# Weight halves of the token mixings written to memory beside an earlier stage, and a new order of the projections

## The chip, the core and the metric

The kernel runs on one core of one Trainium2 chip. The metric is the device time of one execution in microseconds (us). The engines are TensorE (PE, with its weight loads as PEld), VectorE (DVE), ScalarE (ACT), GpSimd (POOL) and SyncE (SP), which here only issues DMAs. All work is in float32; a matmul operand is held as a high part (rounded to the matmul's format) and a low part (the remainder).

## The reference

Two blocks follow one another on one sequence of 512 tokens with 1024 features. The first block is one layer (modulated norms, a gated block MLP beside an mLSTM, then a feed-forward of 4096 with a squared relu). The second is two layers, each with a feed-forward, a token mixing and another feed-forward:

```python
def second_block(x, ...):
    for l in range(DEPTH_2):
        x = x + 0.5 * swiglu(rmsnorm_2(x, ffn1_norm[l]), ...)
        x = x + token_mixing(rmsnorm_2(x, mix_norm[l]), positions, w_in[l], ...)
        x = x + 0.5 * swiglu(rmsnorm_2(x, ffn2_norm[l]), ...)
    return rmsnorm_2(x, final_norm)

def token_mixing(h, ...):
    proj = h @ w_in
    a_part, b_part, c_part = jnp.split(proj, [A_COLS, A_COLS + B_COLS], axis=-1)
    ...
```

The token mixing has three kinds of attention: four dilated heads ("a"), eight latent heads ("m", whose queries and keys come from two small normed latents `cq` and `ckv`), and four differential heads ("d", the difference of two softmaxes, then a head norm). Their outputs are concatenated and multiplied by `w_out`.

## The kernel before

Activations are feature-major: eight tiles of 128 features x 512 tokens. A product of two float32 operands is three matmuls (high x high, high x low, low x high; `mm3`, L246 to 250). A weight unit of 128 x 1024 is loaded into `wraw` (`load_weights`, a ring of 4), and `split_weights` makes the high part with a copy on ACT (L219) and the low part with a subtraction on DVE or, with `pool=True`, on POOL (L220). Both halves stand in one tile `wsp` of 2048 columns, a ring of 3. In the mixings the projections ask for POOL.

The first feed-forward of the first block (`ff`, 64 units of 24 matmuls, 515 to 881 us) loads and splits one unit ahead of each run. It runs inside a region where PE's order is the order of the code; DVE, ACT, POOL and SP are ordered by the scheduler of the tile framework.

`mix(l, ...)` is the token mixing, called once per layer, at about 1243 and 2273 us. Its projections are jobs in the order of the table `JOBS`; the jobs of `FIRST` are done before the first attention tile, and the others fill PE's time between the steps of the tiles (`pieces`, with a budget per tile from `PIECE`). `need` runs jobs at once when a tile lacks its operand. `vd` and `va` are token-major values of the d and a heads; `dq0`, `dk0`, `aq0` and so on are feature-major queries and keys; `kr` is the rotated key, `vb` the latent values, `qk0` to `qk3` the latent queries and keys. The d queries and keys are cut into quadrants on DVE and ACT (`stacked`, L1313 to 1325).

Small products of norms on PE are `toksum` (L306, sums over features), `bc_t` (L313, a transpose) and `bc_b` (L322, a broadcast). Between them lie short DVE steps and one power on POOL (`g_rsqrt`, L293). They belong to chains which emit their next step after a given amount of PE time (the tables `NORM`, `CHAIN`, `INV`), counted by `spend`. An attention tile is scores (`sc`, L1606 for the d heads), a maximum on DVE (`mn`, L1609) which frees the score bank, an exponential on ACT, for d heads the difference (`p`, L1616), a transpose (`ptr`, L1571), its split (`ptl`), and the product with the values (`pv`).

Of the kernel before, what the change touches and what calls it, by code (L numbers as in the profile page):

```python
# [11 lines left out]
F32 = mybir.dt.float32  # L12
# [3 lines left out]
ALU = mybir.AluOpType  # L16
# [56 lines left out]

HEADS = "d0 d1 a0 a1 d2 d3 a2 a3 m0 m1 m2 m3 m4 m5 m6 m7"
MIX_ORDER = [6, 7, 0, 1, 2, 3, 4, 5]
JOBS = "vd dq0 dk0 dq1 aq0 va ak0 dk1 aq1 cq0 cq1 ak1 cq2 ckv0 ckv1 kr vb qk0 qk1 qk2 qk3"
FIRST = "vd dq0 dk0 dq1 aq0"
PIECE = {"d": 2.2, "a": 2.7, "m": 0.6}
STEP = 0.4
LAG = 2  # L80
HEAD0 = 6.5
HEAD = (1.5, 1.0, 2.3, 2.0, 0.6)
ADA0 = 31.0
# [3 lines left out]
CHAIN = (4.0, 4.0, 3.3, 4.5)  # L87
END = (2.0, 1.0)
EARLY = 4
XLP = (0, 1, 2, 3, 4)  # L90
POOL1 = ("q",)
POOL2 = (True, True, False, 3)
# [51 lines left out]
            return e.value  # L144


class Net:
    def __init__(self, ctx, tc, a):
        self.tc, self.nc, self.a = tc, tc.nc, a
        nc = self.nc  # L150
        pool = lambda name, bufs, **k: ctx.enter_context(tc.tile_pool(name=name, bufs=bufs, **k))
        self.cp = pool("const", 1)
        self.wp = pool("weights", 3)
        self.big = pool("big", SLOTS)
        self.tp = pool("tmp", 7)
        self.sp = pool("small", 4)
        self.ps = pool("psum", 1, space=PSUM)
        self.extra, self.within = None, ctx.enter_context(ExitStack())
        self.psb = {"g": 3, "s": 2, "t": 2, "v": 1}
        self.small = "t"  # L160
        self.t, self.chains, self.open_block = 0.0, [], None
        self.last_load = None

        cst = self.cp.tile([P, NCST], F32, name="cst")
# [12 lines left out]
        nc.gpsimd.memset(self.mhalf, -0.5)  # L177
# [110 lines left out]
    def g_rsqrt(self, ss, scale, n, tag=None, eps=EPS):  # L288
        nc = self.nc
        ms, y, t = self.tiny("ms"), self.tiny("y", tag=tag), self.tiny("t")  # L290
        ms, y, t = ms[:, :n], y[:, :n], t[:, :n]
        nc.vector.tensor_scalar(ms, ss, scale, eps, op0=ALU.mult, op1=ALU.add)  # L292
        nc.gpsimd.tensor_tensor(y, ms, self.mhalf[:, :n], op=ALU.pow)  # L293
        yield NORM[2]
        nc.vector.tensor_tensor(t, y, y, op=ALU.mult)
        nc.vector.tensor_tensor(t, t, ms, op=ALU.mult)
        nc.vector.tensor_scalar(t, t, -0.5, 1.5, op0=ALU.mult, op1=ALU.add)
        nc.vector.tensor_tensor(y, y, t, op=ALU.mult)
        return y
# [9 lines left out]
    def g_bcast(self, f8, name, out=None, tag="small", keep=False, tiles=range(NT)):  # L309

        nc = self.nc
        pt = self.bank(tag, "bc_t")
        nc.tensor.transpose(pt[:8, :P], f8, self.c("ident"))  # L313

        self.ft = self.ft[1:] + self.ft[:1]
        ft = self.ft[0]
        nc.vector.tensor_copy(ft[:8], pt[:8, :P])
        nc.vector.tensor_tensor(ft[32:], pt[:8, :P], ft[:8].bitcast(F32), op=ALU.subtract)
        yield NORM[3]
# [12 lines left out]
    def g_bcast4(self, r, name, **k):  # L332
        f8 = self.tiny("f8")
        for h in range(2):
            self.nc.vector.tensor_copy(f8[:, 4 * h:4 * h + 4], r)
        yield NORM[4]
        return (yield from self.g_bcast(f8, name, **k))

    def sq_acc(self, acc, src, first, scale=None):
# [427 lines left out]
    def block1_rest(self, mg):  # L767
# [76 lines left out]
        def gen():  # L844
            yield 2.5
            p0, p1 = self.tok_sum(acc[0]), self.tok_sum(acc[1])
            yield 0.6
            r = yield from self.g_rsqrt(p0, 1.0 / D, NT)
            r2 = self.tiny("r2", 4)
            nc.vector.tensor_tensor(r2, p1, r, op=ALU.mult)  # L850
            nc.vector.tensor_tensor(r2, r2, r, op=ALU.mult)
            rr = yield from self.g_rsqrt(r2, 1.0 / D, NT)
            nc.vector.tensor_tensor(rr, rr, r, op=ALU.mult)
            yield 0.4
            box.rb = yield from self.g_bcast4(rr, "rb2")
# [412 lines left out]
    def mix(self, l, xs, norm, gain):  # L1268


        nc, a = self.nc, self.a
        self.small = "g"
        csc = 96.0 ** -0.5
        mixed, ready = [None] * KT, [False] * KT
        S, scored = {}, [0]

        def get(chain, name):
            while getattr(chain, name) is None:
# [4 lines left out]
        def feature(key, done):  # L1283
            def run(w):
                o = self.bank("g", key)
                yield from self.g_gemm(o, w, xs)
                yield from done(o)
            return lambda: self.weights(a["w2f"][l, FM2_AT[key]], KT, P, pool=True), run

        def scaled(key, factor=1.0):  # L1290

# [35 lines left out]
                S[key] = st  # L1327
            return feature(key, done)

        def values(name, src):  # L1330

            def run(us):
                banks = [self.bank("g", name + "a"), self.bank("g", name + "b")]
# [16 lines left out]
            return lambda: [self.weights(src[i], 4, 256, True) for i in range(2)], run  # L1350

        def latent(name, i, n, gn, last):
            def done(o):
# [41 lines left out]
        def rotated_key():  # L1395
# [9 lines left out]
            def rotation(t):  # L1405
# [5 lines left out]
                for i in range(2):  # L1411
# [5 lines left out]
            def load():  # L1417
                w = self.kilo("wpe", 2)[:, :1024].rearrange("p (k n) -> p k n", k=KT)
                raw = self.load_weights(a["w2f"][l, FM2_AT["kpe"]], KT * P)
                raw = raw.rearrange("p (k n) -> p k n", k=KT)[:, :, :64]  # L1420
                nc.scalar.activation(w[:, :, :64], raw, AF.Copy)
                nc.gpsimd.tensor_tensor(w[:, :, 64:], raw, w[:, :, :64].bitcast(F32), op=ALU.subtract)
                return w

            def run(w):

                o = self.bank("g", "kpe")
# [3 lines left out]
                    self.spend(2 * T * CYCLE)  # L1431
                    yield
                yield from done(o)
            return load, run

        def latent_values():
            def run(w):
# [11 lines left out]
            return lambda: self.weights(a["w2kv"][l], 2, T, pool=True), run  # L1449

        def latent_qk(pr):
            def run(w):
# [25 lines left out]
            return lambda: self.weights(a["w2qk"][l, pr], 1, 1024, pool=True), run  # L1478

        job = {"vd": values("vd", a["w2t"][l, 1]), "va": values("va", a["w2t"][l, 0]), "kr": rotated_key(), "vb": latent_values()}  # L1480
# [44 lines left out]
        def filler():  # L1525
            w = jobs[0][0]()
            for i, (_, run) in enumerate(jobs):
                ahead = jobs[i + 1][0]() if i + 1 < len(jobs) else None
                yield from run(w)
                w = ahead  # L1530
            yield from output()

# [124 lines left out]
        def inverse(pr):  # L1657

            yield INV[0]
            f8 = self.tiny("f8i")  # L1660
            nc.vector.reciprocal(f8, S["sum", pr])
            yield INV[1]
            S["inverse", pr] = yield from self.g_bcast(f8, "fb", tag="t")

        def add_parts(out, o, hh):
# [61 lines left out]
        n = len(tiles)  # L1727
        with self.in_order("ffn"):
            need(*FIRST.split())
        for t in range(-1, n + 3 + LAG + 1):  # L1730

            for lag in (1 + LAG, 1, 0, 1 + LAG, 3 + LAG, LAG, 2 + LAG, -1):
# [194 lines left out]
```

## Time and profile before

| What | Value |
|---|---|
| Median of 3 runs | 2974.22 us (2973.06 to 2974.68) |
| The profiled execution's own time | 2968.44 us |
| Its span, first to last instruction | 2966.7 us |
| PE busy | 2868.8 us (97%) |
| First feed-forward of the first block | 515 to 881 us |
| Head of the first mixing, to the second tile's scores | 1242.7 to 1298.3 us |
| Head of the second mixing, to the second tile's scores | 2272.6 to 2325.5 us |

The span is less than the execution's own time by what lies around the instructions, and the profiled execution is 5.8 us below the median of the runs. A busy PE is not a PE at its peak, since matmuls are pipelined and their ends are modelled; what is read here is the idle time before a matmul, what ended it, and the granted clock of a stretch.

### The profile page before, as it was taken

Reading aid. Unit: us, or ns where it says so; the run is one execution under the profiler, and the core shown is the slowest. Engines: PE = TensorE matmul, PEld = TensorE weight load, DVE = VectorE, ACT = ScalarE, POOL = GpSimd, SP = SyncE. Lnnn points to the kernel's source line nnn. Section 1 sums busy time; section 2 is a strip of 40 time slices with the busy share of each in tenths; the row PEclk is TensorE's granted clock in tenths of the full one; section 3 lists DMA queues with packets and bytes.
Section 4 is the critical chain, followed back from the end, with each engine's and each line's share of the span. In section 5 each row is a group of like instructions: output and inputs, shape, how many; then the busy total and the mean of one; then the engine's idle time right before and its main releaser. Section 6 shows DMA issues by size and latency. Waiting matters only on the chain.

```text
span 2966.7 us, 41470 instructions
## 1 busy us (share of the span) xinstructions
PE 2868.8 (97%) x16251; PEld 2459.4 (83%) x16251; DVE 2030.2 (68%) x3286; ACT 1495.7 (50%) x2527; POOL 417.6 (14%) x255
## 2 busy tenths in 40 slices
PE   6999999999999999989999999999999899999998
PEld 4888977888877999877788999889998777889997
DVE  7766565533448767678768776786775887687675
ACT  5665554422334544467664444444444777544444
POOL 4233340000000000134420000000001344100000
PEclk9999999999999999999999999999999999999999
DMA  6333432222222323211112323323323110133232
GB/s 238 113 122 125 166 111 97 84 95 97 92 93 82 117 91 107 86 65 48 39 43 88 107 95 104 106 87 103 106 90 98 59 51 29 57 96 102 95 106 65
DMA packets 88792, 278.47 MB, mean 94 GB/s; under 512 B 9835, under 2 KB 12139, under 8 KB 88596
## 3 DMA queue, kind: packets, MB, share of 16 engines
q1 hardware_dynamic: 88596, 275.83, 28.1%
q8 instruction: 127, 2.08, 0.3%
q14 instruction: 69, 0.57, 0.1%
HBM read 273.69 MB, written 2.10 MB: 93 GB/s over the span
## 4 chain that ended last, share of the span: by engine, by line
PE 68%; DVE 10%; issue 3%; ACT 3%; DMA 2%; POOL 1%; POOLq 0%; SPq 0%; DVEq 0%; ACTq 0%
PE down L248 5%; PE down L249 5%; PE down L250 5%; PE ff L248 4%; PE ff L250 4%; PE ff L249 4%; PE e L248 4%; PE e L249 4%; PE e L250 4%; PE g L250 2%; PE g L248 2%; PE g L249 2%; PE pv L1589 2%; DMA wraw<-in_w2g 2%; PE ptr L1571 1%
## 5 line engine op out<-in xcount | busy, mean ns | idle before, releaser
L219 ACT ACTIVATE wsp<-wraw 128x1024 fp32r<-128x1024 f32 (+2 forms) x400 | 358.0, 896 | 408.4 <-issue 132.7
L220 DVE TENSOR_TENSOR wsp<-wraw,wsp 128x1024 fp32r<-128x1024 f32 (+2 forms) x334 | 343.8, 1029 | 187.8 <-ACT wsp L219 187.1
L220 POOL TENSOR_TENSOR wsp<-wraw,wsp 128x1024 fp32r<-128x1024 f32 (+1 forms) x66 | 155.7, 2362 | 913.1 <-ACT wsp L219 887.6
L248 PE MATMUL down<-hid,wsp 128*128 128x512 f32 (+1 forms) x712 | 279.2, 392 | 0.0
L250 PE MATMUL down<-hid,wsp 128*128 128x512 f32 (+1 forms) x712 | 279.1, 392 | 0.0
L249 PE MATMUL down<-hid,wsp 128*128 128x512 f32 (+1 forms) x712 | 278.9, 392 | 0.0
L220 DVE TENSOR_TENSOR a<-wraw,a 128x512 fp32r<-128x512 f32 x204 | 134.2, 686 | 138.5 <-ACT a L219 138.5
L219 ACT ACTIVATE a<-wraw 128x512 fp32r<-128x512 f32 x204 | 120.5, 624 | 214.1 <-DMA wraw<-in_w2g 200.8
L293 POOL TENSOR_TENSOR y<-ms,mhalf 128x4 f32<-128x4 f32 (+2 forms) x24 | 27.4, 1140 | 1251.7 <-DVE ms L292 1251.7
L220 DVE TENSOR_TENSOR s<-s,s 128x1024 fp32r<-128x1024 f32 x136 | 163.9, 1217 | 3.9 <-ACT s L219 3.6
L250 PEld LDWEIGHTS down<-hid,wsp 128*128 128x128 f32 x712 | 133.8, 188 | 30.8
L249 PEld LDWEIGHTS down<-hid,wsp 128*128 128x128 f32 x712 | 134.0, 188 | 25.2
L248 PEld LDWEIGHTS down<-hid,wsp 128*128 128x128 f32 x712 | 133.8, 188 | 24.9
L250 PE MATMUL e<-th,s 128*128 128x256 f32 x544 | 152.6, 280 | 0.0
L249 PE MATMUL e<-tl,s 128*128 128x256 f32 x544 | 152.5, 280 | 0.0
L248 PE MATMUL e<-th,s 128*128 128x256 f32 x544 | 152.5, 280 | 0.0
L219 ACT ACTIVATE s<-s 128x1024 fp32r<-128x1024 f32 x136 | 141.1, 1051 | 18.6 <-PE gate L250 6.1
L1115 DVE SCALAR_TENSOR_TENSOR x<-down,x 128x512 f32<-128x512 f32 x158 | 108.1, 684 | 18.2 <-PE down L250 18.0
L447 POOL TENSOR_TENSOR ada<-ada,cb 128x1024 f32<-128x1024 f32 x32 | 84.4, 2651 | 169.4 <-DMA ada<-in_ada 159.0
L249 PEld LDWEIGHTS e<-tl,s 128*128 128x128 f32 x544 | 102.5, 188 | 0.0
L250 PEld LDWEIGHTS e<-th,s 128*128 128x128 f32 x544 | 102.3, 188 | 0.0
L248 PEld LDWEIGHTS e<-th,s 128*128 128x128 f32 x544 | 102.2, 188 | 0.0
(629 smaller groups left out, 8952.0 us busy)
## 6 DMA issues: line engine op xcount, KB each, us to landing
wraw<-in_w2g SPq DMA_DIRECT2D x176, 512.0 KB, 4.1
ada<-in_ada SPq DMA_DIRECT2D x48, 512.0 KB, 5.4
wraw<-in_w2d SPq DMA_DIRECT2D x96, 256.0 KB, 2.7
wraw<-in_w1f SPq DMA_DIRECT2D x44, 512.0 KB, 3.3
wraw<-in_w2d SPq DMA_DIRECT2D x64, 320.0 KB, 3.1
wraw<-in_w1a SPq DMA_DIRECT2D x32, 512.0 KB, 3.2
wraw<-in_w1b SPq DMA_DIRECT2D x32, 512.0 KB, 3.2
wraw<-in_w2f SPq DMA_DIRECT2D x28, 512.0 KB, 3.2
```

The costliest lines, as they stand in the source:

```text
L219: self.nc.scalar.activation(hi, src, AF.Copy)
L220: (self.nc.gpsimd if pool else self.nc.vector).tensor_tensor(lo, src, hi.bitcast(F32), op=ALU.subtract)
L248: mm(out, ah, bh, start=start, stop=False)
L249: mm(out, ah, bl, start=False, stop=False)
L250: mm(out, al, bh, start=False, stop=stop)
L293: nc.gpsimd.tensor_tensor(y, ms, self.mhalf[:, :n], op=ALU.pow)
L447: nc.gpsimd.tensor_tensor(s, s, self.cb, op=ALU.mult)
L1115: nc.vector.scalar_tensor_tensor(x[:, n], o, 0.5, x[:, n], op0=ALU.mult, op1=ALU.add)
L1571: nc.tensor.transpose(tr[:, b * P:(b + 1) * P], p[:, b * P:(b + 1) * P], self.c("ident"))
L1589: nc.tensor.matmul(o, values[b][:, h * P:(h + 1) * P], pt[i][:, b], start=b + i == 0, stop=b + i == NT)
```

## The change

For both layers, the weights of all jobs are loaded and split during the first feed-forward of the first block. A chain `g_parts` starts there after 30 us of PE time and, every 6 us of it, loads one unit, splits it on ACT and DVE into a tile of the `wsp` ring, and stores this tile (1 MB, for the rotated key half of it) to an array `parts` in the device's memory: 46 units. In the mixing `ready_weights` loads a pair of halves from there straight into a `wsp` tile; no split is left for the jobs (the output projection keeps its own).

The order `JOBS` is new, `FIRST` has three jobs instead of five, and `PIECE` moves filler from the a heads to the d heads. A job whose matmuls end before the norm's factor is there leaves its evacuation to a list `late`. The small products use the banks "t" up to the first tile and "g" afterwards (before, "g" all along), and inside the tile loop some of the times of their chains are 1.8 times as long (`SLACK`).

```diff
-JOBS = "vd dq0 dk0 dq1 aq0 va ak0 dk1 aq1 cq0 cq1 ak1 cq2 ckv0 ckv1 kr vb qk0 qk1 qk2 qk3"
-FIRST = "vd dq0 dk0 dq1 aq0"
-PIECE = {"d": 2.2, "a": 2.7, "m": 0.6}
+JOBS = "dq0 vd dk0 aq0 va ak0 dq1 dk1 ckv0 ckv1 aq1 cq0 cq1 cq2 ak1 kr vb qk0 qk1 qk2 qk3"
+FIRST = "dq0 vd dk0"
+PIECE = {"d": 2.4, "a": 2.5, "m": 0.6}
+PARTS = (30.0, 5.0)
...
+    def g_parts(self):
+        yield PARTS[0]
+        for l in range(2):
+            for key, src in mixing_units(self.a, l):
+                for i, s in enumerate(src):
+                    n = len(self.parts_at)
+                    raw, w = self.load_weights(s, 1024), self.kilo("wsp", 2)
...
+                        self.split(w[:, :1024], w[:, 1024:], raw)
+                    yield 1.0
+                    self.nc.sync.dma_start(out=self.parts[n][:, :w.shape[1]], in_=w.bitcast(F32))
+                    self.parts_at[l, key, i] = n
+                    yield PARTS[1]
+
+    def ready_weights(self, l, key, i, nk, n):
+        w = self.kilo("wsp", 2)
+        f = 1024 if key == "kr" else 2048
+        with self.tc.issue_after(self.last_load.ins):
+            self.last_load = self.nc.sync.dma_start(out=w[:, :f].bitcast(F32), in_=self.parts[self.parts_at[l, key, i]][:, :f])
...
     def g_rsqrt(self, ss, scale, n, tag=None, eps=EPS):
-        yield NORM[2]
+        yield NORM[2] * self.slack
...
     def mix(self, l, xs, norm, gain):
-        self.small = "g"
+        self.small = "t"
...
-                yield from done(o)
-            return lambda: self.weights(a["w2f"][l, FM2_AT[key]], KT, P, pool=True), run
+                if norm.rb is None:
+                    late.append(done(o))
+                else:
+                    yield from done(o)
+            return lambda: self.ready_weights(l, key, 0, KT, P), run
...
             need(*FIRST.split())
+        self.small, self.slack = "g", SLACK
```

The order of SyncE at the start of the first feed-forward, before (`w1a`, `w1b` are its own weights):

```order
L229 DMA wraw<-in_w1o 128x1024 x5
L229 DMA wraw<-in_w1a 128x1024 x16
L229 DMA wraw<-in_w1b 128x1024 x16
L229 DMA wraw<-in_w1a 128x1024 x16
L229 DMA wraw<-in_w1b 128x1024 x16
```

and after (`w2f`, `w2t` are weights of the mixings):

```order
L251 DMA wraw<-in_w1o 128x1024 x5
L251 DMA wraw<-in_w1a 128x1024 x6
L251 DMA wraw<-in_w2f 128x1024
L251 DMA wraw<-in_w1a 128x1024
L251 DMA wraw<-in_w2t 128x1024
L251 DMA wraw<-in_w1a 128x1024
L287 DMA parts<-wsp 128x2048
L251 DMA wraw<-in_w2t 128x1024
L251 DMA wraw<-in_w1a 128x1024
L287 DMA parts<-wsp 128x2048
```

After the sixth unit a load of the mixings' weights and a store stand beside each load of the stage's own, and this goes on to the end of the stage.

The order of POOL from the last steps of the first block into the first mixing, before:

```order
L293 TENSOR_TENSOR y<-ms,mhalf 128x4 x3
L220 TENSOR_TENSOR wsp<-wraw,wsp 128x1024 x3
L293 TENSOR_TENSOR y<-ms,mhalf 128x4
L220 TENSOR_TENSOR wsp<-wraw,wsp 128x1024 x9
L1687 TENSOR_TENSOR bias<-bias,cst 128x512 x2
L220 TENSOR_TENSOR wsp<-wraw,wsp 128x1024
```

and after:

```order
L348 TENSOR_TENSOR y<-ms,mhalf 128x4 x4
L1742 TENSOR_TENSOR bias<-bias,cst 128x512 x7
L348 TENSOR_TENSOR y<-ms,mhalf 128x8
L1742 TENSOR_TENSOR bias<-bias,cst 128x512
L348 TENSOR_TENSOR y<-ms,mhalf 128x4
```

The weight splits are gone from POOL; the powers of the norms and the sums of the a heads' biases are left.

The order of DVE ahead of the first score maximum (`ISA p,mn`) in the first mixing, before (`dq` with numbers from 10322 on is `dq1`):

```order
L1313 SCALAR_TENSOR_TENSOR qf<-dq_10322,rb 128x512
L1323 CAST dq_10349<-qf 32x512
L1323 CAST dq_10350<-qf 32x512 x2
L1319 TENSOR_TENSOR dq_10349<-qf,dq_10349 32x512 x2
L1319 TENSOR_TENSOR dq_10350<-qf,dq_10350 32x512 x2
L1325 COPY dq_10350<-dq_10350 32x512
L1294 SCALAR_TENSOR_TENSOR qf<-aq_10374,rb 128x512
L220 TENSOR_TENSOR aq_10401<-qf,aq_10401 128x512
L1609 ISA p,mn<-sc,bias 128x512
```

and after:

```order
L246 SCALAR_TENSOR_TENSOR vd_10525<-vdb,y,vd_10525 128x4x64 x2
L1373 SCALAR_TENSOR_TENSOR qf<-dk_10536,rb 128x512
L1383 CAST dk_10563<-qf 32x512
L1383 CAST dk_10564<-qf 32x512
L1379 TENSOR_TENSOR dk_10563<-qf,dk_10563 32x512 x2
L1379 TENSOR_TENSOR dk_10564<-qf,dk_10564 32x512
L1664 ISA p,mn<-sc,bias 128x512
```

The quadrants of `dq1` and the split of `aq0` have moved behind the first maxima.

## Rows read from the trace of the kernel before

**Rows 1.** Page, part 1: busy us, share of the span and instructions.

```profile
PE 2868.8 (97%) x16251; PEld 2459.4 (83%) x16251; DVE 2030.2 (68%) x3286; ACT 1495.7 (50%) x2527; POOL 417.6 (14%) x255
```

**Rows 2.** Windows: us; busy (x) of PE, PEld, DVE, ACT, POOL; clock, DMA share, GB/s.

```profile
515.00:881.00 366.00, 366.00 (x1616) 297.26 (x1615) 159.61 (x199) 120.23 (x161) 1.01 (x1) 1.00 0.28 92
...
1242.70:1298.30 55.60, 46.91 (x252) 41.03 (x250) 35.11 (x52) 25.25 (x37) 19.45 (x9) 0.90 0.24 82
1298.30:1356.00 57.70, 54.68 (x290) 43.66 (x290) 49.89 (x106) 46.20 (x93) 23.77 (x14) 0.95 0.14 46
...
1422.00:1454.00 32.00, 27.98 (x111) 19.20 (x110) 21.94 (x48) 17.91 (x32) 12.71 (x9) 0.79 0.10 34
...
2272.60:2325.50 52.90, 44.22 (x251) 38.31 (x250) 35.15 (x52) 25.19 (x37) 19.52 (x9) 0.96 0.26 87
2325.50:2449.00 123.50, 115.84 (x607) 90.49 (x606) 106.94 (x229) 95.53 (x192) 51.83 (x31) 0.98 0.15 48
2449.00:2481.00 32.00, 27.98 (x111) 19.35 (x111) 22.20 (x49) 17.97 (x32) 12.77 (x9) 0.79 0.10 33
```

**Rows 3.** Waits of PE, 1242.7 to 1298.3 us: total us, times, longest.

```profile
PE sc L1606 <- DVE mn L1609: 4.9, 1, 4.9
PE vda L248 <- ACT xs L223: 2.3, 2, 1.6
PE vda L250 <- DVE xs L224: 1.5, 2, 1.2
```

**Rows 4.** Waits of PE, 1298.3 to 1454 us.

```profile
PE ptr L1571 <- DVE p L1616: 4.6, 6, 1.6
PE bc_t L313 <- DVE f L335: 2.0, 2, 1.8
...
PE toksum L306 <- DVE vb L224: 1.1, 1, 1.1
```

**Rows 5.** Timeline around the first mixing's start: start, us, engine, line [idle before].

```profile
1238.54 2.39 POOL L220 TENSOR_TENSOR wsp<-wraw,wsp 128x1024 fp32r<-128x1024 f32 x1 [349.12 <-ACT wsp L219]
1239.11 2.38 DVE L224 SCALAR_TENSOR_TENSOR xs<-x,par,xs 128x512 fp32r<-128x512 f32 x1 [0.47 <-ACT xs L223]
...
1245.69 0.75 DVE L224 SCALAR_TENSOR_TENSOR xs<-x,par,xs 128x512 fp32r<-128x512 f32 x1 [0.79 <-ACT xs L223]
...
1256.31 0.16 DVE L296 TENSOR_TENSOR t<-t,ms 128x4 f32<-128x4 f32 x1
```

**Rows 6.** Timeline, 1421 to 1426 us.

```profile
1421.45 2.38 POOL L220 TENSOR_TENSOR wsp<-wraw,wsp 128x1024 fp32r<-128x1024 f32 x1 [0.15 <-ACT wsp L219]
1421.84 2.01 DVE L296 TENSOR_TENSOR t<-t,ms 128x4 f32<-128x4 f32 x1
1425.25 0.27 PE L313 MATMUL bc_t<-cst,f 128*8 128x128 f32 x1 [1.78 <-DVE f L335]
```

**Rows 7.** Timeline: two matmuls of 512 columns in a row.

```profile
1238.54 0.39 PE L248 MATMUL down<-hid,wsp 128*128 128x512 f32 x1
1238.77 0.39 PE L249 MATMUL down<-hid,wsp 128*128 128x512 f32 x1
```

**Rows 8.** Groups: POOL, 1236 to 1610 us; DVE and ACT, 515 to 881 us (mean ns).

```profile
L220 POOL TENSOR_TENSOR wsp<-wraw,wsp 128x1024 fp32r<-128x1024 f32 x25 | 60.6, 2424 | 451.3 <-ACT wsp L219 438.5 <-issue 9.8 <-DVE od L1669 2.9
L220 DVE TENSOR_TENSOR wsp<-wraw,wsp 128x1024 fp32r<-128x1024 f32 x64 | 78.4, 1225 | 70.7 <-ACT wsp L219 70.7
L219 ACT ACTIVATE wsp<-wraw 128x1024 fp32r<-128x1024 f32 x65 | 68.8, 1058 | 143.6 <-PE ff L250 103.5 <-issue 36.2 <-PE ffc L821 3.9
```

**Rows 9.** DMA issues (KB each, median us to landing), and a window at full load.

```profile
wraw<-in_w1a SPq DMA_DIRECT2D x32, 512.0 KB, 3.2
wraw<-in_w2d SPq DMA_DIRECT2D x96, 256.0 KB, 2.7
out<-x SPq DMA_DIRECT2D x2, 384.0 KB, 3.0
12.00:16.00 4.00, 1.87 (x8) 1.78 (x8) 3.42 (x8) 2.35 (x5) 0.46 (x1) 1.00 1.04 420
```

More of the change, by code (lines that the diff above doesn't have):

```diff
@@ L89 @@
 EARLY = 4
+SLACK = 1.8
 XLP = (0, 1, 2, 3, 4)
@@ L144, in drain, with mixing_units @@
             return e.value
+def mixing_units(a, l):
+    out = []
+    for key in JOBS.split():
+        if key in ("vd", "va"):
+            src = [a["w2t"][l, int(key == "vd"), i] for i in range(2)]
+        elif key == "vb":
+            src = [a["w2kv"][l]]
+        elif key[:2] == "qk":
+            src = [a["w2qk"][l, int(key[2])]]
+        else:
+            src = [a["w2f"][l, FM2_AT["kpe" if key == "kr" else key]]]
+        out.append((key, src))
+    return out
 class Net:
@@ L159, in __init__ @@
         self.psb = {"g": 3, "s": 2, "t": 2, "v": 1}
-        self.small = "t"
+        self.small, self.slack = "t", 1.0
         self.t, self.chains, self.open_block = 0.0, [], None
         self.last_load = None
+        n = 2 * sum(len(src) for _, src in mixing_units(a, 0))
+        self.parts, self.parts_at = nc.dram_tensor("parts", (n, P, 2048), F32).ap(), {}
         cst = self.cp.tile([P, NCST], F32, name="cst")
@@ L244, in weights, with split_key @@
         return self.split_weights(self.load_weights(src, nk * n), nk, n, pool)
+    def split_key(self, raw, w):
+        raw = raw.rearrange("p (k n) -> p k n", k=KT)[:, :, :64]
+        self.split(w[:, :, :64], w[:, :, 64:], raw)
+    def g_parts(self):
[5 more added lines that the diff above has]
+                    raw, w = self.load_weights(s, 1024), self.kilo("wsp", 2)
+                    if key == "kr":
+                        w = w[:, :1024]
+                        self.split_key(raw, w.rearrange("p (k n) -> p k n", k=KT))
+                    else:
+                        self.split(w[:, :1024], w[:, 1024:], raw)
[8 more added lines that the diff above has]
+            self.last_load = self.nc.sync.dma_start(out=w[:, :f].bitcast(F32), in_=self.parts[self.parts_at[l, key, i]][:, :f])
+        if key == "kr":
+            return w[:, :1024].rearrange("p (k n) -> p k n", k=nk)
+        return tuple(w[:, h * 1024:h * 1024 + 1024].rearrange("p (k n) -> p k n", k=nk) for h in range(2))
     def mm3(self, out, ah, al, bh, bl, start, stop, **check):
@@ L318, in g_bcast @@
         nc.vector.tensor_tensor(ft[32:], pt[:8, :P], ft[:8].bitcast(F32), op=ALU.subtract)
-        yield NORM[3]
+        yield NORM[3] * self.slack
         pb = self.bank(tag, "bc_b")
@@ L335, in g_bcast4 @@
             self.nc.vector.tensor_copy(f8[:, 4 * h:4 * h + 4], r)
-        yield NORM[4]
+        yield NORM[4] * self.slack
         return (yield from self.g_bcast(f8, name, **k))
@@ L795, in block1_rest @@
         nc.vector.tensor_tensor(fgn, self.par("final1", 0, 8), self.par("ffn1n0", 0, 8), op=ALU.mult)
+        parts = Chain(self, self.g_parts())
         for half in range(2):
@@ L858, in gen @@
             yield from self.g_tables()
+        parts.finish()
         box = Chain(self, gen())
@@ L1271, in mix @@
         nc, a = self.nc, self.a
-        self.small = "g"
+        self.small = "t"
         csc = 96.0 ** -0.5
         mixed, ready = [None] * KT, [False] * KT
-        S, scored = {}, [0]
+        S, scored, late = {}, [0], []
         def get(chain, name):
@@ L1286, in run @@
                 yield from self.g_gemm(o, w, xs)
-                yield from done(o)
-            return lambda: self.weights(a["w2f"][l, FM2_AT[key]], KT, P, pool=True), run
+                if norm.rb is None:
+                    late.append(done(o))
+                else:
+                    yield from done(o)
+            return lambda: self.ready_weights(l, key, 0, KT, P), run
         def scaled(key, factor=1.0):
@@ L1328, in stacked, with values @@
             return feature(key, done)
-        def values(name, src):
+        def values(name):
             def run(us):
@@ L1349, in run @@
                 S[name] = v
-            return lambda: [self.weights(src[i], 4, 256, True) for i in range(2)], run
+            return lambda: [self.ready_weights(l, name, i, 4, 256) for i in range(2)], run
         def latent(name, i, n, gn, last):
@@ L1416, in rotation @@
                     yield 1.5
[L1417 to L1423, printed above, removed]
             def run(w):
@@ L1433, in run @@
                 yield from done(o)
-            return load, run
+            return lambda: self.ready_weights(l, "kr", 0, KT, P), run
         def latent_values():
@@ L1448, in run @@
                 S["vb"] = vb
-            return lambda: self.weights(a["w2kv"][l], 2, T, pool=True), run
+            return lambda: self.ready_weights(l, "vb", 0, 2, T), run
         def latent_qk(pr):
@@ L1477, in run @@
                 yield
-            return lambda: self.weights(a["w2qk"][l, pr], 1, 1024, pool=True), run
-        job = {"vd": values("vd", a["w2t"][l, 1]), "va": values("va", a["w2t"][l, 0]), "kr": rotated_key(), "vb": latent_values()}
+            return lambda: self.ready_weights(l, f"qk{pr}", 0, 1, 1024), run
+        job = {"vd": values("vd"), "va": values("va"), "kr": rotated_key(), "vb": latent_values()}
         for i in range(2):
@@ L1528, in filler @@
                 ahead = jobs[i + 1][0]() if i + 1 < len(jobs) else None
-                yield from run(w)
+                for piece in run(w):
+                    yield piece
+                    while late and norm.rb is not None:
+                        yield from late.pop(0)
                 w = ahead
@@ L1661, in inverse @@
             nc.vector.reciprocal(f8, S["sum", pr])
-            yield INV[1]
+            yield INV[1] * self.slack
             S["inverse", pr] = yield from self.g_bcast(f8, "fb", tag="t")
@@ L1737, in mix @@
             pass
-        self.small = "t"
+        self.small, self.slack = "t", 1.0
         return nx, self.norm(acc)
```

## The prediction

> **What bounds the kernel now.** I read the busy shares first, then the stages by window, then what TensorE (PE) waits for, and last the timeline around the longest waits.
>
> PE is busy 97% of the span, VectorE (DVE) 68%, ScalarE (ACT) 50%, GpSimd (POOL) 14% [rows 1]. So only PE's idle time and its slow clock can be won. In the first feed-forward (515 to 881 us) PE is busy in all of 366 us at full clock, with DVE busy 159.6 us, ACT 120.2 us and the DMA engines 0.28: nothing to win there, but room to put work [rows 2]. The first token mixing (from 1242.7 us) is different. Its head takes 55.6 us with PE busy 46.9 and the granted clock at 0.90 (1.00 is 2.4 GHz, 0.50 is 1.2); a stretch of 32 us later on has the clock at 0.79 [rows 2]. The second mixing (from 2272.6 us) repeats this: 52.9 us and 0.96, then 0.79 again [rows 2].
>
> Who is late: in the head PE waits 4.9 us once for DVE's `mn` (which frees a score bank) and 2.3 and 1.5 us for the last operands `xs` [rows 3]. After it, up to 1454 us, the largest items are 4.6 us for DVE's `p`, 2.0 us for the norm's small product `bc_t`, 1.1 us for `toksum` [rows 4]. The second mixing has the same list.
>
> Why DVE is late: POOL. A multiply-subtract of DVE over 128x512 that takes 0.75 us alone took 2.38 us beside a weight split of POOL that ran from 1238.54 for 2.39 us [rows 5]. At 1421.45 the same happens to a product of 4 columns: 2.01 us instead of 0.16 [rows 5, 6]. That one is part of a norm, so PE's `bc_t` sits idle 1.78 us at 1425.25 [rows 6], and the window with 0.79 of the clock is the one that holds this.
>
> **The change, part by part.** My unit is one matmul of 512 columns: a new one every 0.23 us [rows 7]; 24 of them, a projection or a unit of feed-forward, take 5.57 us.
>
> *Splits removed from the mixing.* POOL has 25 splits of 2.42 us in the first mixing [rows 8]; 3 belong to the output projection and stay, 22 go (and one smaller, of the rotated key). Each costs DVE between nothing and the 1.85 us just read, so 0 to 41 us of DVE time per mixing; it matters only where PE waits for DVE. ACT loses 23 copies of about 1.06 us. PE executes the same products as before.
>
> *New order at the head.* Before, the token-major `vd` came first: its first quarter, 24 half-width matmuls, already wants all eight `xs`. Now `dq0` is first and wants the eighth `xs` at its 22nd matmul, 21 x 0.23 = 4.9 us after the last feed-forward matmul. The chain to it (residual, scaled copy, remainder, each about 0.75 us [rows 5]) takes some 2.5 us without POOL beside it. So the waits of 2.3 and 1.5 us go. The 4.9 us wait for `mn` goes too: ahead of the first `mn` on DVE stood the whole of `dq1` and `aq0`, now only six instructions of `dk0`, though less PE work lies between. I leave 1.5 us for a first wait there.
>
> *The clock.* A stretch of width W at mean clock c carries work that needed (1-c) x W less: head 0.10 x 55.6 = 5.6 us, the next window 0.05 x 57.7 = 2.9, the late window 0.21 x 32 = 6.7; in the second mixing 0.04 x 52.9 = 2.1, 0.02 x 123.5 = 2.5 and 6.7 [rows 2]. Each falls behind waits of PE, so I return it with them.
>
> Sum per mixing. Head: 2.3 + 1.5 + 4.9 = 8.7 of waits, plus 5.6 + 2.9 of clock, less 1.5 and 0.5 left: 15. Second mixing 8.7 + 2.1 + 2.5 - 2 = 11. Late window: 1.8 + 1.1 + 6.7 = 9.6; I take 7 because small products sit there still. Rest: of the 4.6 us behind `p` and about 2 of other small products, half: 3. So 25 and 21, together 46 us. Bounds: nothing (all waits move elsewhere) to 63 (17.2 and 13.3 at the heads, 9.6 twice, 6.6 twice).
>
> *Costs in the mixing.* A projection's weights now come as one transfer of 1 MB straight into a ring of three tiles, and can start only when PE is done with the tile three back. 512 KB land in 3.2 us, 256 KB in 2.7 [rows 9]. For 1 MB: 3.2 + 512 KB at 420 GB/s = 4.5 us, at worst twice 3.2 = 6.4. `dq0` has two units of the last down-projection, 12 x 0.23 x 2 = 5.6 us: hidden at 4.5, 0.8 us late at 6.4. `aq0` has `dk0`'s 5.57 us. I take 1 us per mixing, up to 7. Then, the rest of the `cq` pieces and all of `ak1`, 69 matmuls, are forced in one run ahead of head a2, and seven latent tiles later stand without filler between their scores and transposes: 2 us per mixing, an estimate with no row; 0 to 6. The small products that come later must still be waited for somewhere: 3 per mixing, 0 to 8 (all that [rows 4] hold). Sum 12 for both.
>
> *Costs in the first feed-forward.* 46 loads of 512 KB, 46 ACT copies (1.06 us), 46 DVE remainders (1.23 us) [rows 8] and 46 stores of 1 MB (two of half that), some five parts to six units. DVE goes from 160 to 216 of 366 us, ACT to 169: both hide. DMA: 71 MB more over about 57 units, 318 us: 92 + 224 = 316 GB/s where 420 was reached [rows 2, 9]. What need not hide is the ring of three. Tiles alternate: weights, part, weights. A part may be split only when PE leaves the tile three back; its tile is free for the next weights only when its store has landed. From PE leaving to the weights being ready: ACT's relu 0.6 (half the columns of its copy), ACT 1.06, DVE 1.23, the store L, ACT 1.06, DVE 1.23, gaps 0.5: 5.7 + L. PE allows two units, 11.1 us. So L up to 5.4 us costs nothing, and more costs (L - 5.4)/2 per part. SyncE issues in order, but a store is released by the very remainder that releases the next load, so it goes first. A store of 384 KB lands in 3.0 us [rows 9]. For 1 MB: 3.0 + 640 KB at 420 GB/s = 4.6, or scaled whole 8.0. I take 4.6, since 512 KB against 256 KB shows mostly a fixed part [rows 9], and book 3 us for units with crowded DVE queues; bounds 0 and (8.0 - 5.4)/2 x 46 = 60. The last store is issued about two units before the stage ends, so the next stage's loads behind it on SyncE are in time.
>
> The Trainium skill (DMA: Bandwidth & Descriptors, Anatomy of one DMA) speaks against this part: completion is signalled only after the last byte is confirmed, which it says can be surprisingly long when the target is HBM. Its fixed 2.0 us plus bytes at 436 GB/s would be an estimate of 4.4 us for 1 MB, so hidden; the long delay would be rival 1. [...]
>
> Total: 46 - 12 - 3 = 31 us. The profiled execution took 2968.4 us, its span 2966.7; the median of three runs is 2974.2, 5.8 more. I take the gain from both: 2937 for a profiled one, **2943 us** as median.
>
> **Rivals.**
> 1. *The store lands late in the first feed-forward.* At L = 7 us the ring costs (7 - 5.4)/2 x 46 = 37 us and eats the gain: 2974 - 34 + 37 = 2977, and slower from there on; at L = 8 it is 3000. Decides from L = 6.9. For it: 16 engines that carry 420 GB/s are to carry 320. Against: 3.0 us for 384 KB, and at most three transfers are in flight. The mean of the stage would show PE waiting for ACT or DVE `wsp`. 0.13.
> 2. *The waits only move.* DVE stays the bound of the d heads, where it is busy 49.9 of 57.7 us [rows 2], and gives each gain back at its next product. Then only the waits for `xs` and their clock (2 x 3.8 + 5.6 + 2.1 = 15 us) are won, less 4 for loads and the feed-forward: 2963. For it: DVE's backlog there comes from its own instructions too. Against: the 2.01 us of [rows 6]. 0.15.
> 3. *The halves come late in the mixing.* At 6.4 us and more per load, three jobs per mixing wait 3 us each and the clock falls again as at the head (5 us): 14 per mixing, 2943 + 28 - 2 = 2969. 0.06.
> 4. *The change doesn't do what it says*: part splits slip behind the first feed-forward, and what the mixing gains is lost there: about 2974. The order of SyncE shows the last store ahead of the next stage's loads but one; 0.02.
>
> **How the numbers follow.** Forecast 0.64, rivals 0.13, 0.15, 0.06, 0.02. The range goes from 2920 (a gain of 54: the bound of 63 with the costs at 9) to 2974, leaving out rival 1 and the ends. 0.2% (6 us) is about what a measurement of this kernel tells from no change: faster is below 2968.3. Forecast and rival 2 lie there, less 0.01 of tail: 0.78. Same: rivals 3 and 4 and that tail, 0.09. Slower: rival 1, 0.13.
>
> **What would show it.** Of the changed kernel: the first feed-forward still 366 us with PE never idle, the stores landing within 5.4 us; the mixing's head without a wait for `xs`, clock 1.00; no DVE product of 4 columns above 0.3 us beside POOL; the late window at full clock. Wrong would be: PE waits at `wsp` in the first feed-forward, waits for DMA `wsp<-parts` in the mixing, or the sum of PE's waits per mixing unchanged under other names.

## The result, and the profile after

The changed kernel takes 2940.61 us, median of 4 runs (2938.93 to 2942.15), beside 2973.72 for the kernel before; the ratio is 0.9888, 95% interval 0.9871 to 0.9905. The forecast was 2943 us with a range of 2920 to 2974, and that it would be faster. The time came out as forecast; the experiments show that the reasons behind it were in part wrong, and that half of the change costs time. The kernel with the halves from memory and the order of before takes 0.9812.

The profiled execution has a span of 2940.0 us (page, part 1: busy us, share of the span, instructions; answers [rows 1]):

```profile
PE 2857.1 (97%) x16251; PEld 2451.1 (83%) x16251; DVE 2036.8 (69%) x3332; ACT 1497.9 (51%) x2527; POOL 304.3 (10%) x209
```

Windows, columns as in [rows 2]: first feed-forward; first mixing in three parts (head to the second tile's scores, rest of the d and a heads, latent heads and output); its late window; a short stretch behind the head; the second mixing whole.

```profile
517.20:883.00 365.80, 365.80 (x1615) 297.10 (x1614) 211.76 (x244) 166.85 (x206) 1.01 (x1) 1.00 0.81 287
...
1246.60:1276.90 30.30, 30.30 (x184) 26.66 (x184) 16.22 (x37) 12.45 (x21) 1.01 (x1) 1.00 0.54 196
1276.90:1438.10 161.20, 151.77 (x788) 119.92 (x787) 122.25 (x286) 104.73 (x215) 36.56 (x28) 0.96 0.31 114
1438.10:1559.00 120.90, 117.89 (x649) 96.79 (x648) 84.13 (x132) 77.92 (x154) 25.04 (x17) 1.00 0.14 46
...
1393.00:1437.00 44.00, 38.50 (x175) 27.83 (x174) 29.12 (x63) 24.49 (x47) 17.63 (x14) 0.88 0.32 123
...
1282.80:1286.40 3.60, 3.60 (x20) 3.60 (x19) 3.23 (x8) 2.79 (x7) 0.00 (x0) 0.53 0.00 0
...
2260.60:2573.10 312.50, 300.02 (x1619) 243.40 (x1618) 222.57 (x454) 195.12 (x388) 62.52 (x46) 0.98 0.27 95
```

The feed-forward has PE busy throughout, as before, and the head has lost its waits and its slow clock. Something of both now stands right behind it: PE waits 0.4 us for `mn` and 0.9 for `p` between 1276.9 and 1283 us, and then 3.6 us run at 0.53. The three parts of the mixing of before, in the same cut:

```profile
1242.70:1298.30 55.60, 46.91 (x252) 41.03 (x250) 35.11 (x52) 25.25 (x37) 19.45 (x9) 0.90 0.24 82
1298.30:1452.70 154.40, 143.02 (x715) 109.45 (x714) 128.44 (x276) 112.28 (x222) 63.51 (x38) 0.94 0.14 45
1452.70:1572.40 119.70, 118.50 (x655) 98.59 (x654) 82.76 (x129) 78.22 (x154) 32.13 (x22) 1.00 0.15 49
```

The whole goes from 329.7 to 312.4 us (the second mixing from 327.1 to 312.5). After has fewer matmuls ahead of the second tile, so the first two parts are read as one: 210.0 us before, 191.5 after. The latent part grew by 1.2. What PE waits for in the first mixing of after (total us, times, longest):

```profile
PE vb L303 <- DVE kk L242: 4.5, 1, 4.5
PE pv L1644 <- DVE pair L1724: 2.3, 2, 1.4
PE ptr L1626 <- DVE p L1671: 1.6, 2, 0.9
```

The first is new and sits in the late window, whose clock is still low (0.88). The timeline there (start, us):

```profile
1391.44 2.53 POOL L1742 TENSOR_TENSOR bias<-bias,cst 128x512 f32<-128x512 f32 x2
1391.51 1.25 DVE L350 TENSOR_TENSOR t<-y 128x4 f32<-128x4 f32 x1 [0.18 <-POOL y L348]
...
1408.76 0.69 DVE L1452 SCALAR_TENSOR_TENSOR cs<-bcq,rot 64x512 f32<-64x512 f32 x1
...
1410.52 0.68 DVE L242 TENSOR_TENSOR kk<-krot,kk 64x512 fp32r<-64x512 f32 x1
...
1411.26 0.79 PE L303 MATMUL vb<-wsp,ckv 128*128 128x512 f32 x1 [4.49 <-DVE kk L242]
```

The rotated key `krot` holds one of three banks "g" until its fourth split; four `cs` products of the latent norm stand ahead of that split on DVE, and the latent values `vb` want the bank. That norm was late already: POOL's bias sums held its products of 4 columns to 1.25 us.

### The profile page after: what moved, and what is told of

It reads as the page before. It is cut to its first block, busy times and chain, and to the rows that moved or that the text cites. A ratio compares the mean times of both kernels' runs of the same rounds, so it can differ in the third digit from the quotient of the medians.

```text
span 2940.0 us, 41609 instructions
## 1 busy us (share of the span) xinstructions
PE 2857.1 (97%) x16251; PEld 2451.1 (83%) x16251; DVE 2036.8 (69%) x3332; ACT 1497.9 (51%) x2527; POOL 304.3 (10%) x209
## 4 chain that ended last, share of the span: by engine, by line
PE 71%; DVE 6%; issue 4%; DMA 3%; ACT 2%; POOL 1%; POOLq 0%; SPq 0%; DVEq 0%; ACTq 0%
PE down L304 5%; PE down L305 5%; PE down L303 5%; PE ff L303 4%; PE ff L305 4%; PE ff L304 4%; PE e L303 4%; PE e L305 4%; PE e L304 4%; DMA wraw<-in_w2g 2%; PE g L305 2%; PE pv L1644 2%; PE g L303 2%; PE g L304 2%; PE ptr L1626 2%
## 5 line engine op out<-in xcount | busy, mean ns | idle before, releaser
L242 DVE TENSOR_TENSOR wsp<-wraw,wsp 128x1024 fp32r<-128x1024 f32 (+2 forms) x380 | 404.2, 1066 | 210.3 <-ACT wsp L241 209.5
L305 PEld LDWEIGHTS down<-hid,wsp 128*128 128x128 f32 x712 | 133.7, 188 | 30.6
L1634 ACT ACTIVATE pth<-ptr 128x512 fp32r<-128x512 f32 x128 | 76.3, 596 | 74.9 <-PE ptr L1626 74.4
L1636 DVE TENSOR_TENSOR ptl<-ptr,pth 128x512 fp32r<-128x512 f32 x128 | 87.3, 685 | 20.3 <-ACT pth L1634 19.2
```

The source lines that it names most:

```text
L242: (self.nc.gpsimd if pool else self.nc.vector).tensor_tensor(lo, src, hi.bitcast(F32), op=ALU.subtract)
L1634: nc.scalar.activation(ph[:, :, s], t4, AF.Copy)
L1636: nc.vector.tensor_tensor(pl[:, :, s], t4, ph[:, :, s].bitcast(F32), op=ALU.subtract)
```

## The experiments

To compare the kernels I use the first mixing, from its first projection to the next stage's first `gate`. Its width is PE's idle time plus PE's busy time, and since the matmuls are the same, a longer busy time is a slower clock. All figures but the ratio are from window rows; each ratio is taken against runs of the kernel before that were made along with it. e8 changes the feed-forward only and has its own.

| Kernel | Ratio to before (95%) | Width | PE idle | PE busy | Clock | DVE busy | POOL busy |
|---|---|---|---|---|---|---|---|
| before | 1 | 329.7 | 21.3 | 308.4 | 0.95 | 246.3 | 115.1 |
| after | 0.9888 (0.9871 to 0.9905) | 312.4 | 12.4 | 300.0 | 0.98 | 222.6 | 62.6 |
| e1 | 0.9812 (0.9797 to 0.9826) | 299.1 | 6.5 | 292.6 | 1.00 | 215.3 | 62.9 |
| e2 | 1.0068 (1.0051 to 1.0086) | 337.8 | 29.7 | 308.1 | 0.95 | 242.3 | 114.0 |
| e3 | 0.9877 (0.9858 to 0.9896) | 308.0 | 11.1 | 296.9 | 0.99 | 219.5 | 62.4 |
| e4 | 0.9875 (0.985 to 0.99) | 309.3 | 11.1 | 298.2 | 0.98 | 220.0 | 63.1 |
| e5 | 0.9866 (0.9843 to 0.9888) | 309.3 | 9.8 | 299.5 | 0.98 | 218.3 | 63.3 |
| e6 | 0.9863 (0.9842 to 0.9884) | 309.2 | 8.2 | 301.0 | 0.97 | 214.3 | 63.0 |
| e7 | 0.9942 (0.9923 to 0.9961) | 319.2 | 19.0 | 300.2 | 0.97 | 240.4 | 120.7 |
| e9 | 0.9892 (0.9869 to 0.9915) | 313.3 | 12.9 | 300.4 | 0.98 | 242.4 | 65.8 |
| e10 | 0.9838 (0.9812 to 0.9863) | 305.5 | 9.8 | 295.7 | 0.99 | 215.4 | 63.3 |
| e11 | 0.9826 (0.9807 to 0.9845) | 300.8 | 7.6 | 293.2 | 1.00 | 216.7 | 63.8 |
| e12 | 0.9845 (0.9824 to 0.9865) | 305.9 | 10.4 | 295.5 | 0.98 | 218.6 | 62.9 |

**e1, the halves alone.** The changed kernel with what orders the mixing put back (`PIECE`, the banks of the small products and the evacuations of `late` likewise):

```diff
-JOBS = "dq0 vd dk0 aq0 va ak0 dq1 dk1 ckv0 ckv1 aq1 cq0 cq1 cq2 ak1 kr vb qk0 qk1 qk2 qk3"
+JOBS = "vd dq0 dk0 dq1 aq0 va ak0 dk1 aq1 cq0 cq1 ak1 cq2 ckv0 ckv1 kr vb qk0 qk1 qk2 qk3"
-FIRST = "dq0 vd dk0"
+FIRST = "vd dq0 dk0 dq1 aq0"
...
-SLACK = 1.8
+SLACK = 1.0
```

> Of the change only the halves from memory: the splits leave the mixings (46 loads, splits and stores beside the first feed-forward), but the order of the jobs, the first jobs, the budgets, the banks and times of the small products are those of before. Theory A, POOL's splits beside DVE are what made PE wait: at the head PE waits for xs fall from 3.8 to under 1 us and the wait for mn from 4.9 to 2 us or less, the late window keeps its clock, and two thirds or more of the 33 us are won: 2940 to 2952 us. Theory B, the order did it: vd first still wants all eight xs at once and dq1 and aq0 still stand ahead of the first mn, so the head keeps most of its 15 us; at most 10 us are won: 2963 to 2972 us.

Measured: 2916.76 us. The three parts of its first mixing:

```profile
1245.20:1286.90 41.70, 41.01 (x251) 36.33 (x250) 23.23 (x49) 18.53 (x32) 1.01 (x1) 1.00 0.52 192
1286.90:1425.20 138.30, 133.34 (x717) 103.40 (x715) 109.22 (x276) 99.64 (x206) 33.47 (x26) 1.00 0.27 97
1425.20:1544.30 119.10, 118.23 (x655) 98.78 (x654) 82.88 (x129) 77.38 (x152) 28.41 (x20) 1.00 0.20 70
```

The order is that of before, so the parts compare directly: the head 55.6 to 41.7, the d and a heads 154.4 to 138.3, the rest unchanged. Theory A holds, by more than it said.

**e2, the order alone.** `ready_weights` loads and splits on ACT and POOL as before; no chain `g_parts`.

> Of the change only the order: jobs, first jobs, budgets, late evacuations, banks and times of the small products are those of the changed kernel, but the mixings load and split their weights themselves on ACT and POOL as before, and nothing is stored beside the first feed-forward. Theory A (POOL's splits): at most 10 us are won, 2963 to 2972, with POOL's 2.4 us splits and DVE products lengthened beside them in the head. Theory B (the order): the head loses its waits for xs and mn by itself and two thirds or more are won, 2940 to 2952. If each half of the change gives its part alone, the two gains add up to about 33; if one needs the other, they add up to less.

Measured: 2992.93 us, slower than before; neither theory allowed that. Its head (fewer matmuls, as in after) has 4.9 us of idle time against 8.7. The waits for `xs` and `mn` are gone from it, but PE waits 3.7 us at `toksum` and 1.1 for `dk` instead, and behind it PE waits for other products (1284.0 to 1461.5 us):

```profile
PE vb L304 <- DVE kk L242: 4.5, 1, 4.5
PE sc L305 <- DVE ak L242: 4.1, 2, 2.7
PE ptr L1625 <- DVE p L1670: 3.7, 3, 2.7
PE ptr L1625 <- DVE ptl L1635: 3.4, 2, 3.2
```

The two halves of the change add up: -1.88% and +0.68% make -1.20, measured -1.12, within their intervals.

**e3, the small products not later** (`SLACK = 1.0` in the changed kernel).

> The changed kernel with the factor 1.8 on the small products' times set to 1. Theory: these times matter little, since a small product that comes sooner finds its vector ready once POOL's splits are gone: 2938 to 2945 us, no wait of PE at bc_t or bc_b above 1 us. Rival: without the factor the small products come before their vectors: PE waits at toksum, bc_t and bc_b grow by 3 to 8 us per mixing, 2947 to 2957.

Measured: 2935.36 us, not to be told from the changed kernel, and just below the range of the theory. The waits are those of the rival: the theory allowed none above 1 us, and PE waits 4.4 us once at `bc_t` and 1.7 in all at `bc_b`, where the changed kernel has 0.3 and 0.5.

```profile
PE bc_t L368 <- DVE w L1669: 4.4, 1, 4.4
```

In return the wait at `vb` falls from 4.5 to 1.0 us, so PE's idle time goes from 12.4 to 11.1 us only.

**e4, one job moved.**

```diff
-... ckv0 ckv1 aq1 cq0 cq1 cq2 ak1 kr vb ...
+... ckv0 ckv1 aq1 cq0 cq1 ak1 cq2 kr vb ...
```

> The changed kernel with one job moved: ak1 stands ahead of cq2 in the order of jobs. cq2 (24 matmuls) is no longer forced ahead of the head a2, the rotated key and the latent values come later and apart, and the first latent tiles get filler again. Theory: in the late window PE waits 4.5 us for the splits of the rotated key because these hold one of three banks while the latent values want it, and the clock falls to half for 10.2 us behind that; and the first latent tiles run without filler, which costs 4.7 us against before. Both go: 4.5 + 4 + 3 per mixing, about 2918 to 2925 us. Rival: DVE and ACT are the bound of the a heads there and the wait moves to another product: 2936 to 2944 us.

Measured: 2936.43 us: the rival by its time. The wait of 4.5 us at `vb` is gone, but PE waits 2.1 at `bc_t`, 1.7 at `toksum` and 1.3 at `bc_b`, and its idle time falls by 1.3 us only. So freeing the bank did not free PE. That DVE's backlog is the cause and found another place is the likely reading, but it is argued, not shown: the new order of the jobs may bring waits of its own.

**e5 and e6, parts of the order on top of e1.** e5 has the new `PIECE`, e6 the banks and times of the small products.

> The kernel of e1 (halves from memory, all else as before; it took 2916.8 us) with the new budgets alone: 2.4 us of filler per tile of the d heads and 2.5 of the a heads. Theory: of the new order it is the sequence of jobs that costs 24 us (cq and ak1 forced ahead of a2, rotated key and latent values side by side), and the budgets by themselves cost nothing: 2912 to 2921 us. Rival: the budgets take filler from the a heads and cost 8 us or more: 2925 to 2940.

> The kernel of e1 (2916.8 us) with the small products as in the changed kernel: banks t up to the first tile, g afterwards, their times 1.8 as long within the tile loop. Theory: with the old order their vectors are ready early, so that later products change nothing or give back the 3 to 5 us that PE waits at bc_t, bc_b and toksum per mixing: 2908 to 2919 us. Rival: later products hold the banks g and the latent norms longer, and what waits for those norms comes late: 2924 to 2935.

Measured: 2930.08 and 2929.56 us, both in the range of the rival; the mechanisms that the rivals give were not tried apart. Each alone costs about 0.5% against e1, and of the 10 us that the first mixing grows, idle time is 3.3 and 1.7, the rest clock. The prices do not add up: the two together would make 1.05%, and the whole order, new jobs included, costs 0.76% (after against e1); e3, which is without the later times, costs 0.65%. The price of the table `JOBS` by itself stays open; it was not tried alone.

**e7 and e10, POOL's or ACT's work put back on top of e1**, behind each load of halves, into a tile that nobody reads:

```diff
+        idle = self.wp.tile([P, 1024], F32, name="idle", tag="wraw", bufs=WBUFS[0])
+        h = f // 2
+        self.nc.gpsimd.tensor_tensor(idle[:, :h], w[:, :h].bitcast(F32), w[:, h:f].bitcast(F32), op=ALU.subtract)
```

(in e10 the last line is `self.nc.scalar.activation(idle[:, :h], w[:, :h].bitcast(F32), AF.Copy)`).

> The kernel of e1 (2916.8 us) with POOL's work put back, and nothing else: for each of the 23 loads of halves per mixing POOL subtracts one half from the other into a tile that nobody reads (128 x 1024, for the rotated key half of that). ACT's copies stay away, and PE never waits for these. Theory: what the splits cost before was DVE, lengthened beside POOL; then this kernel gives back most of the 58 us, 2950 to 2975, with DVE's 0.7 us products at up to 2.4 us and waits of PE for mn, p and xs back. Rival: the gain came from something else, the weights' readiness or ACT's copies: 2914 to 2925.

> The kernel of e1 (2916.8 us) with ACT's copies put back instead of POOL's subtractions: for each load of halves in the mixings ACT copies one half into a tile that nobody reads (1.06 us each). POOL's work put back gave 37 of the 58 us back, so 21 are open. Theory: they are ACT's copies, which stand ahead of exponentials and transposed halves: 2925 to 2937. Rival: ACT has room, they cost nothing, and the 21 us come from PE and DVE waiting for the splits' results or from the clock: 2914 to 2921.

Measured: 2953.76 and 2922.08 us. POOL's work gives back 1.30 of 1.88%, ACT's 0.26 (its interval overlaps e1's); if the prices add up, which was not tried, 0.3 is left for what needs the splits' results. In e7 (the first mixing, POOL's group there, PE's longest wait):

```profile
1239.10:1558.30 319.20, 300.18 (x1618) 242.61 (x1618) 240.36 (x454) 195.93 (x388) 120.70 (x69) 0.97 0.26 93
```
```profile
L299 POOL TENSOR_TENSOR idle<-wsp 128x1024 f32<-128x1024 f32 (+1 forms) x23 | 57.0, 2480 | 434.6 <-DVE xs L246 354.2 <-DMA wsp<-parts 80.2
```
```profile
PE sc L1658 <- DVE mn L1661: 6.0, 1, 6.0
```

The wait for `mn` of [rows 3] is back, with nobody waiting for POOL's result, and DVE is busy 25.0 us longer than in e1 with the same instructions. PE's only wait for POOL itself is 1.0 us for `qq`. That POOL's own small powers stand in its queue behind this work, and so make DVE's norms late, was not tried apart.

**e8, a longer store.**

```diff
+                    self.nc.sync.dma_start(out=self.again[n], in_=w[:, :1024].bitcast(F32))
```

> The changed kernel with a second store of each part's high half (512 KB, to an array that nobody reads) right behind the first, so that a tile of the ring of three comes free later: traffic of the first feed-forward 344 instead of 287 GB/s. By the sum of the prediction the landing that frees a tile goes from 4.8 to about 6.1 us, the ring allows 5.4, and each of 46 parts costs (6.1 - 5.4)/2: the first feed-forward takes 382 instead of 366 us, the whole about 2957. Rival: the ring has more slack than the sum gave it, PE is never idle there, and the time stays within 3 us of 2941.

Measured: 2955.42 us, 0.9946 (0.9932 to 0.9961). DMA issues (KB each, median us to landing), first of after, then of e8, with e8's first feed-forward and PE's waits there:

```profile
parts<-wsp SPq DMA_DIRECT2D x44, 1024.0 KB, 4.8
wraw<-in_w1a SPq DMA_DIRECT2D x32, 512.0 KB, 4.8
```
```profile
parts<-wsp SPq DMA_DIRECT2D x44, 1024.0 KB, 6.1
```
```profile
515.50:900.10 384.60, 372.46 (x1615) 296.51 (x1614) 211.23 (x244) 167.28 (x206) 1.01 (x1) 1.00 0.89 336
```
```profile
PE ff L307 <- DVE wsp L243: 7.0, 12, 1.5
PE ff L305 <- ACT wsp L242: 5.1, 6, 1.2
```

ACT's splits wait there for tiles that a store holds (total us, times, longest; 64.3 us in after, where PE waits for none of them):

```profile
ACT wsp L242 <- DMA parts<-wsp: 77.9, 30, 5.2
```

The second store did not run behind the first: it needs only ACT's high half, so SyncE issues it ahead (at 609.62 and 610.89 us, for example), and the tile still comes free with the 1 MB store, which now lands later. The stage takes 384.6 us where the sum said 382; of the 18.8 us more, 12.1 are idle time of PE and the rest is modelled busy time. The loads land later too (`in_w1a` 5.8 us), but ACT waits only 4.1 us for loads of weights, so the ring held the splits and not the loads. So 4.8 us is hidden and 6.1 is not: the cover is thin.

**e9, the splits on DVE** in the kernel before (`pool=True` and its like dropped in the jobs).

> The kernel before with the 23 splits of each mixing's jobs on DVE instead of POOL; nothing is stored beside the first feed-forward, the order is that of before. DVE gets 22 x 1.23 = 27 us more of its own per mixing and loses the 1.85 us per split at most (41) by which POOL held it up. Theory: POOL's holding of DVE is what cost, and DVE's own splits cost DVE about as much as POOL did in sum but in pieces of 1.2 us: 2955 to 2972 us, a part of the 58 us, the rest needs the splits to leave the mixing. Rival: DVE has no room for 27 us more beside the heads and PE waits longer: 2980 to 3000.

Measured: 2940.57 us, as fast as the whole change and below both forecasts. Its first mixing:

```profile
1244.10:1557.40 313.30, 300.39 (x1619) 242.09 (x1618) 242.40 (x477) 215.22 (x410) 65.80 (x46) 0.98 0.17 54
```

DVE is as busy as before (242.4 and 246.3), and yet PE's idle time falls from 21.3 to 12.9 us. So it is not how much DVE has to do. DVE's groups of 1240 to 1460 us, first of before, then of e9, last of e7 (mean ns behind the comma):

```profile
L1609 DVE CUSTOM_DVE_ANT_0 p<-sc,bias 128x512 f32<-128x512 f32 x32 | 20.7, 680 | 2.0 <-PE sc L1606 2.0
L1616 DVE SCALAR_TENSOR_TENSOR p<-p,w 128x512 f32<-128x512 f32 x16 | 15.6, 977 | 0.1
```
```profile
L1609 DVE CUSTOM_DVE_ANT_0 p<-sc,bias 128x512 f32<-128x512 f32 x32 | 20.7, 680 | 1.3 <-PE sc L1606 1.3
L1616 DVE SCALAR_TENSOR_TENSOR p<-p,w 128x512 f32<-128x512 f32 x16 | 12.6, 788 | 0.2
```
```profile
L1668 DVE SCALAR_TENSOR_TENSOR p<-p,w 128x512 f32<-128x512 f32 x16 | 16.6, 1038 | 0.2
```

The product `p` of two operands in SBUF drops from 977 to 788 ns without POOL's splits and takes 1038 in e7 with POOL's idle work; the score maxima, which read their scores from PSUM, stay at 680. The Trainium skill (SBUF — State Buffer, Who interferes with whom) says that a DVE instruction with two SBUF inputs contends with a GpSimd instruction that reads SBUF, and that one with at most one SBUF input, outside the 2-port perf modes, does not. The rows agree.

**e11 and e12, around e1.** e11 has `PIECE = {"d": 2.0, "a": 2.9, "m": 0.6}`. e12 adds `for _ in range(5): nc.vector.tensor_copy(t, pk)` ahead of the rotated key's splits.

> The kernel of e1 (2916.8 us) with the budgets moved against the change's direction: 2.0 us of filler per tile of the d heads (2.2) and 2.9 of the a heads (2.7). The change's direction cost 13 us in e5. Theory: the old order was tuned to its budgets, and any shift puts small products beside DVE's queues: 2922 to 2935. Rival: the d heads want less filler, since DVE is their bound: 2905 to 2916.

> The kernel of e1 (2916.8 us) with five copies of 0.69 us more on DVE once per mixing, between the rotated key's product and its splits, where PE already waits 1.2 us at the latent values: PE waits some 3.4 us longer there, once per mixing. Theory: such a wait costs more than itself, because the clock falls to half behind it: 3.4 us plus 2 to 7 us of half-clock loss per mixing, 2928 to 2938 in all, with half-clock stretches of 3.4 to 13.7 us in the records which e1 hardly has. Rival: a wait costs what it lasts, 2921 to 2925, with the clock as in e1.

Measured: 2920.42 us for e11, not to be told from e1, so neither side shows there. 2925.80 us for e12, between the two forecasts; its ratio is 0.33% above that of e1, which beside the same run of before is 9.8 us for the two waits, and the intervals just overlap (up to 0.9826, from 0.9824). The records say more: PE's wait in the first and in the second mixing, and three stretches at half clock (two of the first mixing, one of the second):

```profile
PE vb L303 <- DVE vb L246: 5.4, 1, 5.4
```
```profile
PE vb L303 <- DVE vb L246: 4.9, 1, 4.9
```
```profile
1404.00:1407.40 3.40, 3.40 (x14) 2.65 (x13) 1.28 (x5) 0.00 (x0) 1.65 (x1) 0.50 0.02 5
1417.20:1421.00 3.80, 3.31 (x8) 2.20 (x9) 2.53 (x6) 1.16 (x2) 0.00 (x0) 0.50 0.00 0
2424.70:2434.00 9.30, 8.88 (x30) 6.38 (x31) 5.85 (x12) 4.75 (x9) 0.00 (x0) 0.50 0.32 115
```

In e1 that wait is 1.2 us in either mixing, and the clock behind it 1.00. The first mixing grew by 6.8 us: 3.9 idle, 2.9 slower matmuls. Not all of the 2.9 belongs to the wait: the first stretch lies ahead of the five copies, behind a wait of 0.7 us at `toksum` that e1 has too, there at 1.00. The other two stretches lie behind the long wait. Matmuls that keep PE busy 3.3 and 8.9 us at half clock have lost half of that, by estimate 1.7 and 4.4 us. In the profiled execution a wait thus costs more than it lasts, as the theory said, in the first mixing by less than it gave.

## Why the prediction was right, and where it was not

*What bounds.* Right: PE's waits for DVE, DVE held by POOL, and the clock behind the waits. e7 and e9 show the holding, and e12 the clock behind one wait.

*The head* (15 us). The size was about right: the head alone gave 13.9 by e1, in the old order, where 12 stood for it (the 15 also counts 2.9 of clock behind the head). The reason given first was wrong: the waits for `xs` and `mn` did not need `dq0` at the front or the shorter `FIRST`. The step read "without POOL beside it" and booked the gain under the order. The 1.5 us left for a first wait came, as 0.4 and 0.9 us, with 3.6 us at 0.53 behind them.

*The late window* (7 us) failed. Idle time and clock cost 4.0 + 6.7 = 10.7 us before [rows 2] and 5.5 + 0.12 x 44 = 10.8 after. The waits of [rows 4] left or shrank (`p` from 4.6 to 1.6 us), the wait at `vb` came: rival 2 in this one place. The forecast "no product of 4 columns above 0.3 us" failed too, since POOL's bias sums stayed.

*The sum of the gains* (46 us, bounds 0 to 63) was too small: with the old order the halves alone give 1.88% of 2973.7 us, 56 us net of their loads (30.6 in the first mixing, 26.3 in the second by the windows, where 25 and 21 stood). The d and a heads with the late window are the larger part of this: they gave 16.1 in the first mixing of e1 where 3 + 7, and the 2.9 of clock booked under the head, stood.

*The costs in the mixing* (12 us). The loads land in 4.8 us (forecast 4.5) and PE waits for none in either mixing of after. The latent part lost 1.2 us (forecast 2). The cost of the order as a whole was too small: after against e1 it is 0.76%, 23 us, where some 10 stood (12 less the loads). I looked for its cost at two named places, and e5 and e6 show a third to a sixth of it as idle time and the rest as clock. Where in DVE's queue it begins was followed for the late window only.

*The first feed-forward* (3 us). Right: 365.8 us, cost nothing. The store takes 4.8 us (forecast 4.6). The estimate of 4.4 from the Trainium skill (DMA: Bandwidth & Descriptors, Anatomy of one DMA) is near that too, though the Trainium skill gives that fit for DMAs that GpSimd issues, and these are SyncE's. The long delay for writes to memory that it names shows in no row here. e8 bears out the ring's arithmetic at 6.1 us with 18.8 us against 16. Rival 1 did not come, but its mechanism is real. Its price at L = 7, 2977 us, is within 6 us of before, so by the prediction's own rule it belonged under "same" there and not under "slower".

So 46 - 12 - 3 = 31 was a gain 10 too small and a cost some 10 too small, and the two errors cancel. That 2940.61 came so near to 2943 is luck.

## What to carry to other kernels

A share of POOL's work can be dear although POOL is busy for 14% of the span only (35% of the first mixing): look which DVE instructions with two operands in SBUF lengthen beside it, and try the same work on DVE first, which here gave the whole gain of the change with five edits. When a change has several halves, run them apart, because one can pay for the other. In this kernel, where the clock fell behind PE's waits, they cost about twice their length in all.

## What the runs showed of the hardware

A 512 KB load takes 3.2 us in the first feed-forward of before [rows 9] and 4.8 us (5.6 for `in_w1b`) at 287 GB/s beside the stores; at 336 GB/s, in e8, the stage waited for its stores. In the first mixing, 14.8 us less idle time came with 15.9 us less busy time for the same matmuls (before against e1): about half of what the waits cost there is the clock. In e12 the clock is at 0.50 for 3.8 us from the end of one wait of 5.4 us, and for 9.3 us from the end of one of 4.9, where e1, with waits of 1.2 us, has 1.00. A 128x512 product of two SBUF operands on DVE takes 788 ns on the mean without POOL's splits, 977 with them and 1038 beside POOL's idle work; a maximum with its scores in PSUM takes 678 to 683 in all of these.
